# Attention scores taken in pairs of an even and an odd head, with two PSUM banks for each step

## The chip, the cores and the metric

One core of a Trainium2 chip runs the whole program. The metric is the device time of one execution in microseconds (us). Engines are named as the profile names them: PE is the matrix engine (TensorE), DVE the vector engine, ACT the scalar engine, POOL GpSimd, SP the queue that issues the weight loads.

## The reference, cut to what matters

Two layers, 256 tokens, model width 1024, all in float32. In each layer the stretch that concerns us stands between two SwiGLU blocks:

```
h = rms_norm(x);  qa,ka,va, qb,kb,vb, xc,gc = split(h @ w_in)
A: 4 query heads on 2 key/value heads, rotary, window 128, a sink per head
B: 6 heads, rotary, three dilated windows combined by their softmax denominators
C: causal conv(4) -> gated linear recurrence (scan), times gelu(gc)
x = x + concat(A, B, C) @ w_out
```

Heads have 64 channels. Scores are `q . k * 64**-0.5`, masked, and go through a softmax; the mixture of the three windows of B is done with an added mask, so that each head of A and of B needs one score matrix of 256 queries by the keys up to them.

## The kernel before, in words

Weights come from memory as float32 and are split in two parts (`piece`, L128 to L132): ACT writes a rounded part `hi`, DVE the rest `lo`. Each weight product is then three matmuls (hi·hi, hi·lo, lo·hi). There are 7 pairs of such buffers, so a split waits until PE has used an older pair.

The mixing stretch of a layer (`mixer`) is written as a list of steps, `PLAN`, which is walked once per layer. A step `xc`, `qb`, `kb`, `vb`, `pa`, `gc` is a projection by a slice of w_in (`pa` gives q, k and v of A); `cg`, `cs`, `co` are the gates, the scan and the end of C. `B1s0` is the 0th score step of B for the second half of the queries (half 1, which sees 256 keys; half 0 sees 128); `B1p0` multiplies a piece of its softmax by the values; `B1f` divides by the sum and transposes. `woB` and `woCA` are the output projection of the finished parts. A scheduler reorders the instructions of each engine when the program is built, but buffers of one pool are handed out in the order of the list. Once built, the order on each engine is fixed, and each engine takes its instructions in that order.

Scores (`Attend.scores`, L826 to L840): a head's q and k lie transposed, with its 64 channels on one half of the 128 rows, an even head of B on the lower half and an odd one on the upper (for A the two key/value heads). A score step takes up to 512 columns of PSUM, one bank: 2 heads of half 1, or 4 (for B 3) of half 0, all from the same half of the rows. PE writes the scores to the bank; DVE reads it once per head, adds the mask and finds the maximum (L830), which empties the bank; DVE makes the negative maximum (L834 or L836), and ACT the exponential and its sum (L839). `pv` (L850 to L856) transposes the softmax on PE, ACT copies it to SBUF, and PE multiplies by the values into the tile `o`.

PSUM banks: 4 with the tag `mm` (projections, `wout`), 2 with the tag `at` (scores, `o`, one of the three tiles of `xc` and of `gc`, the gates), 2 with the tag `tp` (transposes).

Of the kernel before, what the change touches and what calls it, by code (L numbers as in the profile page):

```python
# [11 lines left out]
F32 = mybir.dt.float32  # L12
F32R = mybir.dt.float32r
I32 = mybir.dt.int32
AF = mybir.ActivationFunctionType
ALU = mybir.AluOpType

P = 128

PLAN = ("xc qb kb cg B1s0 vb B0s0 B0s1 B0p0 B0p1 pa B1s2 B1s1 cs A0s0 B1s3 B1p0 B0f A0s1 B1p2 B1p1 A1s0 B1p3 "  # L20
        "A1s1 A0p1 A0p0 gc A1p0 B1f woB A1p1 A0f A1f co woCA").split()

TAG_GATE, TAG_SCORES, TAG_O, TAG_WO = 'at', 'at', 'at', 'mm'
TAG_XC, TAG_GC = ('mm', 'at', 'mm'), ('at', 'mm', 'mm')

BUFS = 5, 14, 4, 2, 2, 8, 4
# [8 lines left out]
NEG = -3.0e38  # L35
# [3 lines left out]
def hybrid_trunk(ctx: ExitStack, tc: tile.TileContext, a: dict, out: bass.AP):  # L39
    nc = tc.nc  # L40
    x = a["x"]
    S, D = x.shape[1], x.shape[2]
    L = a["w_in"].shape[0]
    DFF = a["ffn1_gate"].shape[2]
    HD = 64
    HF = HD // 2
    AQ, AKV, BH = 4, 2, 6
# [5 lines left out]
    SC = HD ** -0.5  # L53
# [6 lines left out]
    act = ctx.enter_context(tc.tile_pool(name="act", bufs=1))  # L60
# [18 lines left out]
    KC = KD // HC  # L79
# [67 lines left out]
    K = {}  # L147
# [489 lines left out]
    def mixer(l, norm, nxt):  # L637
        V, G, A = nc.vector, nc.gpsimd, nc.scalar
# [5 lines left out]
        NP = BH // 2  # L644
# [70 lines left out]
        n = CT * (S + NTAP)  # L715
# [92 lines left out]
        class Attend:  # L808


            def __init__(self, h, heads, vs, mask, sinks):
                self.h, self.heads, self.vs, self.mask, self.sinks = h, heads, vs, mask, sinks
                self.nk = (h + 1) * P
                self.nh = sum(len(b) for b in heads)
                st = act.tile([P, 4, 8], F32, tag="st", bufs=4, name="st")
                self.mx, self.nm, self.ls, self.ri = (st[:, i] for i in range(4))
                self.slot = [sum(len(b) for b in heads[:i]) for i in range(len(heads))]
                self.sm = [None] * len(heads)
                self.ob = None

            def scores(self, gi):
                group, j, nk, mx, nm = self.heads[gi], self.slot[gi], self.nk, self.mx, self.nm
                h, n = self.h, len(group)
                sb = bank(TAG_SCORES, "scores")
                for s, (i, g, q, k) in enumerate(group):
                    nc.tensor.matmul(sb[:, s * nk:(s + 1) * nk], q[g * HD:(g + 1) * HD, h * P:(h + 1) * P],  # L826
                                     k[g * HD:(g + 1) * HD, :nk], start=True, stop=True)
                sm = act.tile([P, 512], F32, tag="sm", bufs=NSM, name="sm")
                for s in range(n):
                    V.tensor_tensor_reduce(out=sm[:, s * nk:(s + 1) * nk], in0=sb[:, s * nk:(s + 1) * nk],  # L830
                                           in1=self.mask, scale=1.0, scalar=NEG, op0=ALU.add, op1=ALU.max,
                                           accum_out=mx[:, j + s:j + s + 1])
                if self.sinks is None:
                    V.tensor_scalar(nm[:, j:j + n], mx[:, j:j + n], -SC, None, op0=ALU.mult)  # L834
                else:
                    V.scalar_tensor_tensor(nm[:, j:j + n], mx[:, j:j + n], -SC, self.sinks[1][:, j:j + n],  # L836
                                           op0=ALU.mult, op1=ALU.min)
                for s in range(n):
                    A.activation(sm[:, s * nk:(s + 1) * nk], sm[:, s * nk:(s + 1) * nk], AF.Exp, scale=SC,  # L839
                                 bias=nm[:, j + s:j + s + 1], accum_out=self.ls[:, j + s:j + s + 1])  # L840
                self.sm[gi] = sm

            def pv(self, gi):
                h, sm = self.h, self.sm[gi]
                if self.ob is None:
                    self.ob = bank(TAG_O, "o")
                tp = bank("tp", "pT")
                n = len(self.heads[gi]) * self.nk
                for b in range(n // P):
                    nc.tensor.transpose(tp[:, b * P:(b + 1) * P], sm[:, b * P:(b + 1) * P], ident)  # L850
                pT = act.tile([P, 512], F32, tag="pT", bufs=2, name="pT")
                copy("pT", pT[:, :n], tp[:, :n])
                for s, (i, g, q, k) in enumerate(self.heads[gi]):
                    for kb in range(h + 1):
                        b = s * (h + 1) + kb
                        nc.tensor.matmul(self.ob[:, i * HD:(i + 1) * HD], pT[:, b * P:(b + 1) * P], self.vs[kb][i],  # L856
                                         start=(kb == 0), stop=(kb == h))

            def finish(self):
                nh, ls, ri, ob, mx = self.nh, self.ls, self.ri, self.ob, self.mx  # L860
                if self.sinks is not None:
                    V.tensor_tensor(mx[:, :nh], self.sinks[0], self.nm[:, :nh], op=ALU.add)
                    A.activation(mx[:, :nh], mx[:, :nh], AF.Exp)
                    V.tensor_tensor(ls[:, :nh], ls[:, :nh], mx[:, :nh], op=ALU.add)
                V.reciprocal(ri[:, :nh], ls[:, :nh])
                o = scratch(nh * HD, "o")
                order = [i for group in self.heads for i, *_ in group]
                if order == list(range(nh)):
                    V.tensor_tensor(o.rearrange("p (n d) -> p n d", d=HD),
                                    ob[:, :nh * HD].rearrange("p (n d) -> p n d", d=HD),  # L870
                                    ri[:, :nh, None].to_broadcast([P, nh, HD]), op=ALU.mult)
                else:

                    v = lambda z: z[:, :nh * HD].rearrange("p (n g d) -> p g n d", g=2, d=HD)
                    V.tensor_tensor(v(o), v(ob), ri[:, :nh].rearrange("p (g n) -> p g n", g=2)[:, :, :, None]
                                    .to_broadcast([P, 2, nh // 2, HD]), op=ALU.mult)
                return o


# [3 lines left out]
        va, vb = [], []  # L883
# [11 lines left out]
        def a_attend(h):  # L895
            t = C["qkA"]
            heads = [[(g * AG + r_, g, t[:, r_], t[:, AG]) for r_ in range(AG)] for g in range(AKV)]
            sl = slice(l * AQ, (l + 1) * AQ)
            return Attend(h, heads, va, K["mA"][h], (K["sink"][:, sl], K["nsink"][:, sl]))

        def b_in(j):
            dst = QB[j][:, :NP * S].rearrange("p (c t) -> p c t", c=NP)
# [12 lines left out]
        def b_attend(h, q, k):  # L915
            hd = lambda i: (i, i % 2, q[:, i // 2], k[:, i // 2])
            per = 512 // ((h + 1) * P)
            heads = []
            for g in range(2):
                for i0 in range(0, NP, per):  # L920
                    heads.append([hd(2 * i + g) for i in range(i0, min(i0 + per, NP))])
            return Attend(h, heads, vb, K["mB"][h], None)

        def out_stage(ks, last):

            for c in range(HC):
                w = {}
                for k0, n in ks:
                    w.update(zip(range(k0, k0 + n), by_columns(w_out, k0, n, c)))
                n = len(w)  # L930
                w = list(w.items())
                bs = [bank(TAG_WO, "wout")[:, :S] for _ in range(KC)]
                order = [(i, j) for i in range(n - LO) for j in range(KC)]
                order += [(i, j) for j in range(KC) for i in range(n - LO, n)]
# [17 lines left out]

        for step in PLAN:
            nm, arg = step[:2], step[2:]
# [22 lines left out]
            else:  # L977
                g, h = nm[0], int(nm[1])
                t = C[g][h]
# [4 lines left out]
                else:  # L984
                    k, n = R[g]
# [37 lines left out]
```

## Time and profile before

| | |
|---|---|
| three runs | 945.01, 946.7, 946.91 us; median 946.7 |
| the profiled execution | 946.71 us, of which the trace spans 944.9 |
| mean granted clock of PE | 0.996 of full speed |
| PE busy | 935.2 us, 99% |
| DVE, ACT, POOL busy | 662.1 us (70%), 502.0 us (53%), 59.8 us (6%) |
| the two mixing stretches, about | 192 to 293 us and 654 to 755 us |

A busy time is what an engine spent between the start and the end of its instructions. PE's instructions are pipelined: a row of 0.39 us may be followed by the next after 0.23 us, so a cost is best read from one start to the next. [...]

### The profile page before, as it was taken

What the parts mean: (1) busy time and instruction counts of PE and PEld (TensorE: products, weight loads), DVE (VectorE), ACT (ScalarE), POOL (GpSimd) and SP (SyncE); (2) the same over time, 40 slices, a digit from 0 to 9 for tenths busy, and PEclk for the clock granted to TensorE, in tenths of its full rate; (3) what the DMA queues carried; (4) which work ended last, traced back from release to release, by engine and by line L of the source; (5) the groups of instructions that cost most, each with busy time, mean ns of one, the idle gap of its engine ahead of it and who ended that gap; (6) DMA issues with size and microseconds to landing.
All of it is one profiled execution on the core that took longest, in us unless ns stands there. A gap on an engine that the chain in (4) does not pass through costs nothing.

```text
span 944.9 us, 18771 instructions
## 1 busy us (share of the span) xinstructions
PE 935.2 (99%) x7572; PEld 910.7 (96%) x7572; DVE 662.1 (70%) x1155; ACT 502.0 (53%) x769; POOL 59.8 (6%) x107
## 2 busy tenths in 40 slices
PE   8999999999999999999999999999999999999997
PEld 8999999999899999999999999999988999999886
DVE  6786675989678867765577766565995975656544
ACT  7554554455667545555355555544475675555530
POOL 4000001011102000001000000011100100000000
PEclk9999999999999999999999999999999999999999
DMA  8876665655246666565746666654741755666631
GB/s 279 238 227 206 191 197 162 195 175 166 79 132 214 178 205 198 180 216 165 223 157 200 194 205 203 202 180 119 224 138 50 229 178 180 196 207 201 201 112 44
DMA packets 134408, 171.13 MB, mean 181 GB/s; under 512 B 5822, under 2 KB 106258, under 8 KB 134322
## 3 DMA queue, kind: packets, MB, share of 16 engines
q1 hardware_dynamic: 133184, 168.32, 58.0%
q0 software_dynamic: 528, 0.57, 0.4%
q8 instruction: 59, 0.97, 0.4%
q10 hardware_dynamic: 608, 1.06, 0.4%
q14 instruction: 29, 0.22, 0.1%
HBM read 168.88 MB, written 1.05 MB: 180 GB/s over the span
## 4 chain that ended last, share of the span: by engine, by line
PE 97%; issue 1%; DMA 1%; SPq 0%; DVE 0%; POOLq 0%; POOL 0%
PE gate L461 9%; PE gate L462 9%; PE gate L463 8%; PE up L462 8%; PE up L463 8%; PE up L461 8%; PE down L461 6%; PE down L463 6%; PE down L462 6%; PE down L609 2%; PE down L608 2%; PE down L607 2%; PE scores L826 2%; PE wout L938 2%; PE wout L939 2%; PE wout L940 2%
## 5 line engine op out<-in xcount | busy, mean ns | idle before, releaser
L132 DVE TENSOR_TENSOR lo<-raw,hi 128x1024 fp32r<-128x1024 f32 (+2 forms) x334 | 388.8, 1173 | 113.7 <-ACT hi L130 113.3
L130 ACT ACTIVATE hi<-raw 128x1024 fp32r<-128x1024 f32 (+2 forms) x334 | 335.5, 1017 | 167.4 <-PE down L462 60.9
L461 PE MATMUL gate<-x,hi 128*128 128x256 f32 x704 | 195.8, 278 | 0.5 <-ACT x L372 0.5
L462 PE MATMUL gate<-x,hi 128*128 128x256 f32 x704 | 195.1, 277 | 0.0
L461 PE MATMUL up<-x,hi 128*128 128x256 f32 x704 | 194.6, 277 | 0.0
L462 PE MATMUL up<-x,hi 128*128 128x256 f32 x704 | 194.5, 277 | 0.0
L463 PE MATMUL gate<-x,lo 128*128 128x256 f32 x704 | 194.5, 277 | 0.0
L463 PE MATMUL up<-x,lo 128*128 128x256 f32 x704 | 194.1, 276 | 0.0
L461 PE MATMUL down<-g,hi 128*128 128x256 f32 x528 | 145.8, 276 | 0.0
L462 PE MATMUL down<-g,hi 128*128 128x256 f32 x528 | 145.7, 276 | 0.0
L463 PE MATMUL down<-g,lo 128*128 128x256 f32 x528 | 145.6, 276 | 0.0
L461 PEld LDWEIGHTS gate<-x,hi 128*128 128x128 f32 x704 | 132.6, 188 | 0.7 <-ACT x L372 0.7
L462 PEld LDWEIGHTS gate<-x,hi 128*128 128x128 f32 x704 | 132.8, 189 | 0.0
L462 PEld LDWEIGHTS up<-x,hi 128*128 128x128 f32 x704 | 132.4, 188 | 0.0
L463 PEld LDWEIGHTS gate<-x,lo 128*128 128x128 f32 x704 | 132.3, 188 | 0.0
L461 PEld LDWEIGHTS up<-x,hi 128*128 128x128 f32 x704 | 132.3, 188 | 0.0
L463 PEld LDWEIGHTS up<-x,lo 128*128 128x128 f32 x704 | 132.0, 188 | 0.0
L136 ACT ACTIVATE g<-gu 128x256 fp32r<-128x256 f32 x88 | 36.6, 417 | 149.3 <-DVE gu L475 125.4
L461 PEld LDWEIGHTS down<-g,hi 128*128 128x128 f32 x528 | 99.1, 188 | 0.1
L462 PEld LDWEIGHTS down<-g,hi 128*128 128x128 f32 x528 | 99.1, 188 | 0.0
L463 PEld LDWEIGHTS down<-g,lo 128*128 128x128 f32 x528 | 99.0, 188 | 0.0
L474 DVE TENSOR_TENSOR gu<-up,half 128x256 f32<-128x256 f32 x66 | 27.7, 421 | 47.1 <-PE up L463 47.1
(228 smaller groups left out, 1325.5 us busy)
## 6 DMA issues: line engine op xcount, KB each, us to landing
raw<-ffn_down SPq DMA_DIRECT2D x88, 512.0 KB, 4.5
raw<-ffn_gate SPq DMA_DIRECT2D x87, 512.0 KB, 4.7
raw<-ffn_up SPq DMA_DIRECT2D x87, 512.0 KB, 5.2
raw<-w_in SPq DMA_DIRECT2D x40, 384.0 KB, 3.7
raw<-w_out SPq DMA_DIRECT2D x12, 512.0 KB, 3.7
raw<-w_in SPq DMA_DIRECT2D x8, 512.0 KB, 4.6
raw<-w_out SPq DMA_DIRECT2D x8, 256.0 KB, 2.8
xr<-x SPq DMA_DIRECT2D x4, 256.0 KB, 4.6
```

What stands on the lines that cost most here:

```text
L130: nc.scalar.activation(hi[:, :m], raw[:, :m], AF.Copy)
L132: nc.vector.tensor_tensor(lo[:, :m], raw[:, :m], hi[:, :m].bitcast(F32), op=ALU.subtract)
L136: nc.scalar.activation(hi, v, AF.Copy)
L461: nc.tensor.matmul(b, wh, both[:, :S], start=first, stop=False)
L462: nc.tensor.matmul(b, wh, both[:, S:], start=False, stop=False)
L463: return nc.tensor.matmul(b, wl, both[:, :S], start=False, stop=last)
L474: V.tensor_tensor(u, bs[1], half, op=ALU.mult)
L607: nc.tensor.matmul(b, gh, wh, start=first, stop=False)
L608: nc.tensor.matmul(b, gh, wl, start=False, stop=False)
L609: return nc.tensor.matmul(b, gl, wh, start=False, stop=last)
L826: nc.tensor.matmul(sb[:, s * nk:(s + 1) * nk], q[g * HD:(g + 1) * HD, h * P:(h + 1) * P], k[g * HD:(g + 1) * HD, :nk], start=True, stop=True)
L938: nc.tensor.matmul(bs[j], wi, PT[:, k, 0], start=(i == 0), stop=False)
```

## The change

The score step now takes pairs: for each pair of an even and an odd head of B (for A, a head from each key/value head) one score matrix goes to a first bank and the other to a second one, and the matmuls are written alternately, one from the lower half of the rows and one from the upper. Half 1 of B has now 2 steps in place of 4, half 0 has 1 in place of 2, and each half of A has 1 in place of 2: 5 steps a layer in place of 10. Each step asks for two `at` banks at once. The softmax tiles hold the heads in their natural order, so `pv` takes B's half 0 in tiles of 4 and 2 heads, and `finish` needs no reordering. The tile `o` comes from the `mm` banks in place of `at`, and `wout` from two `at` and two `mm` banks in place of four `mm`. `PLAN` is rewritten for the new steps.

```
-PLAN = ("xc qb kb cg B1s0 vb B0s0 B0s1 B0p0 B0p1 pa B1s2 B1s1 cs A0s0 B1s3 B1p0 B0f ...
+PLAN = ("xc qb kb cg B1s0 vb B0s0 B0p0 B0p1 pa B1s1 cs A0s0 B1p0 B0f B1p1 A1s0 B1p2 A0p0 gc ...
-TAG_GATE, TAG_SCORES, TAG_O, TAG_WO = 'at', 'at', 'at', 'mm'
+TAG_GATE, TAG_SCORES, TAG_O, TAG_WO = 'at', 'at', 'mm', ('at', 'at', 'mm', 'mm')
...
             def scores(self, gi):
-                sb = bank(TAG_SCORES, "scores")
-                for s, (i, g, q, k) in enumerate(group):
-                    nc.tensor.matmul(sb[:, s * nk:(s + 1) * nk], q[g * HD:(g + 1) * HD, h * P:(h + 1) * P],
-                                     k[g * HD:(g + 1) * HD, :nk], start=True, stop=True)
...
+                sb = [bank(TAG_SCORES, "scores") for _ in banks]
+                at = {}
+                for s in range(max(len(b) for b in banks)):
+                    for t, group in zip(sb, banks):
+                        if s < len(group):
+                            i, g, q, k = group[s]
+                            at[i] = t[:, s * nk:(s + 1) * nk]
+                            nc.tensor.matmul(at[i], q[g * HD:(g + 1) * HD, h * P:(h + 1) * P],
+                                             k[g * HD:(g + 1) * HD, :nk], start=True, stop=True)
...
+                order = [i for t in tiles for i in t]
+                for i in order:
+                    V.tensor_tensor_reduce(out=p[i], in0=at[i], in1=self.mask, scale=1.0, scalar=NEG, op0=ALU.add,
+                                           op1=ALU.max, accum_out=mx[:, i:i + 1])
...
         def b_attend(h, q, k):
...
+            for i0 in range(0, NP, per):
+                pairs = range(i0, min(i0 + per, NP))
+                banks = [[hd(2 * i + g) for i in pairs] for g in range(2)]
+                idx = range(2 * i0, 2 * pairs[-1] + 2)
+                steps.append((banks, [list(idx[i:i + per]) for i in range(0, len(idx), per)]))
...
-                bs = [bank(TAG_WO, "wout")[:, :S] for _ in range(KC)]
+                bs = [bank(TAG_WO[j], "wout")[:, :S] for j in range(KC)]
```

On PE, where the projection `vb` ends and `pa` follows (the same in both layers), the order changes as follows; `x2` and the like count equal instructions in a row:

```order
 L428 MATMUL vb<-lo,x 128x384
 L430 MATMUL vb<-hi,x 128x384
+L830 MATMUL scores<-mixed 128x256 x4
+L830 MATMUL scores<-mixed 128x128 x6
+L830 MATMUL scores<-mixed 128x256 x2
+L856 MATMUL pT<-ident,sm 128x128 x6
+L862 MATMUL o<-vb,pT 128x64 x4
 L427 MATMUL pa<-hi,x 128x512
 L428 MATMUL pa<-lo,x 128x512
```

All scores of B, the transposes of the softmax of half 0 and four of its value products now stand ahead of the first matmul of `pa`. Before, `pa` followed `vb` at once, and these stood among the matmuls of `pa` and `gc`.

The same place in the changed program, one by one, with the buffers' numbers and with the semaphores that an instruction waits for:

```order
L430 MATMUL vb_2974<-hi_3006,x_2522 128x384
L830 MATMUL scores_2944<-mixed_2597 128x256 [waits DVE_49,Activation_49]
L830 MATMUL scores_2945<-mixed_2597 128x256 [waits Activation_49]
L830 MATMUL scores_2944<-mixed_2597 128x256
L830 MATMUL scores_2945<-mixed_2597 128x256
L830 MATMUL scores_3039<-mixed_2597 128x128 [waits DVE_49]
L830 MATMUL scores_3039<-mixed_2597 128x128 x2
L830 MATMUL scores_3040<-mixed_2597 128x128 [waits DVE_49]
L830 MATMUL scores_3040<-mixed_2597 128x128 x2
L830 MATMUL scores_3187<-mixed_2597 128x256 [waits DVE_49]
L830 MATMUL scores_3188<-mixed_2597 128x256 [waits DVE_49]
```

Three steps of two banks each stand in a row, and there are two `at` banks: the second and the third step wait for DVE to have read the step before. The first step alternates between its two banks, the second was left as three and three.

On PE at the end of `pa`, in both layers:

```order
-L427 MATMUL pa<-hi,x 128x512
-L428 MATMUL pa<-lo,x 128x512
-L850 MATMUL pT<-ident,sm 128x128
-L430 MATMUL pa<-hi,x 128x512
-L850 MATMUL pT<-ident,sm 128x128
+L805 MATMUL qkT<-ident,r 128x128 x3
+L830 MATMUL scores<-mixed 128x128 x4
+L805 MATMUL qkT<-ident,r 128x128 x2
+L856 MATMUL pT<-ident,sm 128x128 x4
+L805 MATMUL qkT<-ident,r 128x128
+L437 MATMUL gT<-ident,o 128x128 x3
+L830 MATMUL scores<-mixed 128x256 x4
```

Before, the projection `gc` began right after `pa` and the transposes `qkT` of A's rotated q and k came some 30 matmuls later. Now `qkT` and the scores of A follow `pa` directly, and `gc` comes behind them.

On DVE in the changed program, between the reading of the first score step and that of the second:

```order
L839 ISA sm_2951,st_2916<-scores_2945,mB1_2235 128x256
L839 ISA st_2916 128x1
L757 TENSOR_TENSOR mixed_2597<-mixed_2597 128x768
L843 TENSOR_SCALAR st_2916<-st_2916 128x4
L760 SCALAR_TENSOR_TENSOR mixed_2597<-mixed_2597 128x256
L760 SCALAR_TENSOR_TENSOR mixed_2597<-mixed_2597 128x256
L839 ISA sm_3047,st_2915<-scores_3039,mB0_2208 128x128
```

L757 and L760 belong to the recurrence of C (L760 is its scan); up to the first reading of scores DVE's order is the same in both programs. What moved here is that two splits of weights (`lo`) that stood among these before now come later.

## Rows read from the trace of the kernel before

**Rows 1.** The page: busy time by engine; the chain that ended last, by engine

```profile
PE 935.2 (99%) x7572; PEld 910.7 (96%) x7572; DVE 662.1 (70%) x1155; ACT 502.0 (53%) x769; POOL 59.8 (6%) x107
PE 97%; issue 1%; DMA 1%; SPq 0%; DVE 0%; POOLq 0%; POOL 0%
```

**Rows 2.** Busy time in a stretch: length, each engine, granted clock, DMA share, GB/s

```profile
230.00:246.00 16.00, 16.00 (x83) 13.00 (x82) 14.52 (x40) 11.25 (x25) 0.73 (x2) 1.00 0.39 122
```

**Rows 3.** Timeline of PE: start, length, engine, line, tiles, shape, count (merged)

```profile
230.04 0.39 PE L427 MATMUL pa<-hi,x 128*128 128x512 f32 x1
...
232.19 1.80 PE L826 MATMUL scores<-mixed 64*128 64x256 f32 x10
233.92 0.51 PE L427 MATMUL pa<-hi,x 128*128 128x512 f32 x1
```

**Rows 4.** Timeline of DVE, first layer

```profile
234.43 0.41 DVE L830 CUSTOM_DVE_ANT_0 sm<-scores,mB 128x256 f32<-128x256 f32 x1
...
234.77 0.41 DVE L830 CUSTOM_DVE_ANT_0 sm<-scores,mB 128x256 f32<-128x256 f32 x1
...
237.74 0.96 DVE L757 TENSOR_TENSOR mixed<-mixed 128x768 f32<-128x768 f32 x1 [0.97 <-ACT mixed L756]
238.61 0.16 DVE L834 TENSOR_SCALAR st<-st 128x3 f32<-128x3 f32 x1
...
239.83 1.84 DVE L760 TENSOR_TENSOR_SCAN mixed<-mixed 128x256 f32<-128x256 f32 x3
241.59 0.26 DVE L830 CUSTOM_DVE_ANT_0 sm<-scores,mB 128x128 f32<-128x128 f32 x1
...
241.78 0.28 DVE L830 CUSTOM_DVE_ANT_0 sm<-scores,mB 128x128 f32<-128x128 f32 x1
```

**Rows 5.** Timeline of ACT, first layer

```profile
243.58 0.40 ACT L839 ACTIVATE sm<-sm,st 128x128 f32<-128x128 f32 x1 [0.84 <-DVE st L834]
...
243.98 0.39 ACT L839 ACTIVATE sm<-sm,st 128x128 f32<-128x128 f32 x1
...
253.09 0.60 ACT L657 ACTIVATE pT<-pT 128x512 f32<-128x512 f32 x1
```

**Rows 6.** Timeline of PE, later in the first layer

```profile
259.19 0.71 PE L826 MATMUL scores<-mixed 64*128 64x128 f32 x4
259.83 0.44 PE L850 MATMUL pT<-ident,sm 128*128 128x128 f32 x2
...
262.14 0.61 PE L850 MATMUL pT<-ident,sm 128*128 128x128 f32 x4
262.68 1.13 PE L826 MATMUL scores<-mixed 64*128 64x256 f32 x4
263.74 1.10 PE L856 MATMUL o<-va,pT 128*128 128x64 f32 x8
```

**Rows 7.** Timelines of PE and DVE, second layer

```profile
692.06 0.39 PE L427 MATMUL pa<-hi,x 128*128 128x512 f32 x1
...
697.85 0.42 DVE L830 CUSTOM_DVE_ANT_0 sm<-scores,mB 128x256 f32<-128x256 f32 x1
```

**Rows 8.** Timeline of DVE, the end of `pa` in the first layer

```profile
243.57 0.35 DVE L661 TENSOR_SCALAR va<-pa,rstd 128x128 f32<-128x128 f32 x1
...
245.01 0.34 DVE L661 TENSOR_SCALAR va<-pa,rstd 128x128 f32<-128x128 f32 x1
...
246.51 1.21 DVE L132 TENSOR_TENSOR lo<-raw,hi 128x1024 fp32r<-128x1024 f32 x1
249.35 0.56 DVE L659 COPY mixed<-qkT 128x384 f32<-128x384 f32 x1 [1.63 <-PE qkT L805]
```

**Rows 9.** Busy time in stretches at the start of the span

```profile
8.00:10.00 2.00, 0.90 (x7) 0.90 (x7) 1.65 (x4) 1.08 (x3) 0.00 (x0) 0.91 0.93 314
10.00:12.00 2.00, 2.00 (x11) 2.00 (x11) 1.80 (x4) 0.84 (x1) 0.00 (x0) 0.50 0.87 261
12.00:14.00 2.00, 2.00 (x15) 2.00 (x15) 2.00 (x3) 2.00 (x6) 0.00 (x0) 0.73 1.09 368
```

More of the change, by code (lines that the diff above doesn't have):

```diff
@@ L18 @@
 P = 128
-PLAN = ("xc qb kb cg B1s0 vb B0s0 B0s1 B0p0 B0p1 pa B1s2 B1s1 cs A0s0 B1s3 B1p0 B0f A0s1 B1p2 B1p1 A1s0 B1p3 "
-        "A1s1 A0p1 A0p0 gc A1p0 B1f woB A1p1 A0f A1f co woCA").split()
-TAG_GATE, TAG_SCORES, TAG_O, TAG_WO = 'at', 'at', 'at', 'mm'
+PLAN = ("xc qb kb cg B1s0 vb B0s0 B0p0 B0p1 pa B1s1 cs A0s0 B1p0 B0f B1p1 A1s0 B1p2 A0p0 gc B1f A1p0 A0f woB "
+        "A1p1 A1f co woCA").split()
+TAG_GATE, TAG_SCORES, TAG_O, TAG_WO = 'at', 'at', 'mm', ('at', 'at', 'mm', 'mm')
 TAG_XC, TAG_GC = ('mm', 'at', 'mm'), ('at', 'mm', 'mm')
@@ L808, in mixer, with __init__ @@
         class Attend:
-            def __init__(self, h, heads, vs, mask, sinks):
-                self.h, self.heads, self.vs, self.mask, self.sinks = h, heads, vs, mask, sinks
+            def __init__(self, h, steps, vs, mask, sinks):
+                self.h, self.steps, self.vs, self.mask, self.sinks = h, steps, vs, mask, sinks
                 self.nk = (h + 1) * P
-                self.nh = sum(len(b) for b in heads)
+                self.nh = sum(len(b) for banks, _ in steps for b in banks)
@@ L815, in __init__ @@
                 st = act.tile([P, 4, 8], F32, tag="st", bufs=4, name="st")
                 self.mx, self.nm, self.ls, self.ri = (st[:, i] for i in range(4))
-                self.slot = [sum(len(b) for b in heads[:i]) for i in range(len(heads))]
-                self.sm = [None] * len(heads)
+                self.sm = []
                 self.ob = None
             def scores(self, gi):
-                group, j, nk, mx, nm = self.heads[gi], self.slot[gi], self.nk, self.mx, self.nm
-                h, n = self.h, len(group)
@@ L824, in scores @@
-                sb = bank(TAG_SCORES, "scores")
-                for s, (i, g, q, k) in enumerate(group):
-                    nc.tensor.matmul(sb[:, s * nk:(s + 1) * nk], q[g * HD:(g + 1) * HD, h * P:(h + 1) * P],
-                                     k[g * HD:(g + 1) * HD, :nk], start=True, stop=True)
[L828 to L832, printed above, removed]
+                (banks, tiles), nk, mx, nm, h = self.steps[gi], self.nk, self.mx, self.nm, self.h
@@ new lines, in scores @@
+                p = {}
+                for tile_heads in tiles:
+                    sm = act.tile([P, 512], F32, tag="sm", bufs=NSM, name="sm")
+                    p.update((i, sm[:, s * nk:(s + 1) * nk]) for s, i in enumerate(tile_heads))
+                    self.sm.append((sm, tile_heads))
+                order = [i for t in tiles for i in t]
+                for i in order:
+                    V.tensor_tensor_reduce(out=p[i], in0=at[i], in1=self.mask, scale=1.0, scalar=NEG, op0=ALU.add,
+                                           op1=ALU.max, accum_out=mx[:, i:i + 1])
@@ L833, in scores @@
+                sl = slice(min(order), max(order) + 1)
                 if self.sinks is None:
-                    V.tensor_scalar(nm[:, j:j + n], mx[:, j:j + n], -SC, None, op0=ALU.mult)
+                    V.tensor_scalar(nm[:, sl], mx[:, sl], -SC, None, op0=ALU.mult)
                 else:
[L836 to L840, printed above, removed]
@@ L841, in scores @@
-                self.sm[gi] = sm
+                    V.scalar_tensor_tensor(nm[:, sl], mx[:, sl], -SC, self.sinks[1][:, sl], op0=ALU.mult, op1=ALU.min)
+                for i in order:
+                    A.activation(p[i], p[i], AF.Exp, scale=SC, bias=nm[:, i:i + 1], accum_out=self.ls[:, i:i + 1])
             def pv(self, gi):
-                h, sm = self.h, self.sm[gi]
+                h, (sm, heads) = self.h, self.sm[gi]
                 if self.ob is None:
@@ L847, in pv @@
                 tp = bank("tp", "pT")
-                n = len(self.heads[gi]) * self.nk
+                n = len(heads) * self.nk
                 for b in range(n // P):
@@ L852, in pv @@
                 copy("pT", pT[:, :n], tp[:, :n])
-                for s, (i, g, q, k) in enumerate(self.heads[gi]):
+                for s, i in enumerate(heads):
                     for kb in range(h + 1):
@@ L866, in finish @@
                 o = scratch(nh * HD, "o")
[L867 to L876, printed above, removed]
+                V.tensor_tensor(o.rearrange("p (n d) -> p n d", d=HD),
+                                ob[:, :nh * HD].rearrange("p (n d) -> p n d", d=HD),
+                                ri[:, :nh, None].to_broadcast([P, nh, HD]), op=ALU.mult)
                 return o
@@ L898, in a_attend @@
             sl = slice(l * AQ, (l + 1) * AQ)
-            return Attend(h, heads, va, K["mA"][h], (K["sink"][:, sl], K["nsink"][:, sl]))
+            per = 512 // ((h + 1) * P)
+            return Attend(h, [(heads, [list(range(i, i + per)) for i in range(0, AQ, per)])], va, K["mA"][h], (K["sink"][:, sl], K["nsink"][:, sl]))
         def b_in(j):
@@ L917, in b_attend @@
             per = 512 // ((h + 1) * P)
[L918 to L922, printed above, removed]
+            steps = []
+            for i0 in range(0, NP, per):
[3 more added lines that the diff above has]
+                steps.append((banks, [list(idx[i:i + per]) for i in range(0, len(idx), per)]))
+            return Attend(h, steps, vb, K["mB"][h], None)
         def out_stage(ks, last):
```

## The prediction

> **What bounds the kernel now.** I read the page first. PE is busy 99% of the span, and the chain that ended last runs on PE for 97% of it [rows 1]. The busy time by stretch says the same of the place of the change: from 230 to 246 us PE is busy 16.00 of 16.00 us at a granted clock of 1.00, while DVE is busy 14.52 [rows 2]. So whatever shortens PE's own work is gained in full, whatever makes PE wait is lost in full, and DVE is nearly full just where the scores begin. The timelines of PE and DVE show how these two stand to each other. PE ends `vb` and starts `pa` at 230.04 us, and makes the first scores of B at 232.19 [rows 3]; DVE reads the first of these only at 234.43 [rows 4], because it is behind. In the second layer `pa` starts at 692.06 and DVE reads the first scores at 697.85 [rows 7]. Before, PE had the matmuls of `pa` and `gc` to go on with, so that this lag cost nothing. DVE's order up to that first reading is the same in the changed program, and what it works on there comes from before the end of `vb`; so I keep 234.43 and 697.85 as the times at which it can start to empty the first score banks, however early PE fills them.
>
> **What PE's own work loses.** A score run of four records takes 0.64 us with 128 columns and 1.06 us with 256 [rows 6], and the run of 4 wide and 6 narrow records 1.73 us, from 232.19 to 233.92 [rows 3]. The three together give 0.112 us a narrow record, 0.217 a wide one and 0.19 fixed for a run. Ahead of the run at 262.68, four transposes of 0.11 us from 262.14 would have been over at 262.58, so another 0.1 is lost on entering. About 0.3 us for a run, then. Before there are 9 runs a layer (the first holds two steps); the order now shows 3. Six fewer, in two layers: 12 x 0.3 = 3.6 us saved. The number of scores, transposes and value products is unchanged, and I cost the moves of `o` and `wout` between banks at nothing: in the output projection no wait of PE is seen before, and the chain from the last `gc` to the split of C has all of `woB` to hide behind. If that cover failed it would cost under 1 us a layer.
>
> **The first wait it adds.** Between `vb` and `pa`, PE now has three score steps, six transposes and four value products in a row, and only two `at` banks. Counted from T, the first reading by DVE, the chain to the first matmul of `pa` is: four readings of wide scores at 0.34 us, 1.37 from start to start [rows 4]; L757, 0.87, and a small operation, 0.1; two scans at 1.76 / 3 = 0.59, 1.17; three readings of narrow scores at about 0.2, 0.6 (the first bank of the second step is free); the third scan, 0.59; three more readings, 0.6; the negative maximum, 0.2. DVE is done with the second step at T + 5.5. ACT then makes six exponentials at 0.40, 2.4, and copies the first four transposed tiles, 0.60 [rows 5]; PE makes four value products in eight records of 0.11, 0.9 (eight in 1.10 with the tail [rows 6]). Sum 9.4, with the hand-overs 9.5. `pa` starts at 234.43 + 9.5 = 243.9, in place of 230.04: 13.9 us later. In these PE does 2.0 us (first step), 1.6 (second), 1.15 (third), 0.66 (transposes) and 0.9 (values) = 6.3. It idles 7.6 us. In the second layer T is 5.79 us behind the end of `vb`, in place of 4.39, and the idle time is 9.0. Behind the waiting scores stand all of `pa` and `gc`, whose weights are there: nothing of this can be taken ahead, since PE takes its list in order.
>
> **The second wait.** Behind `pa` there is no more `gc` to go on with. The transposes of A's q and k need the rotation, and A's scores need DVE's copy of them. DVE begins as the first half of `pa` is done, about 0.5 us before the end of all (the last record of that half stands four places from the end at 0.23, and lasts 0.39). Then it has scaling and rotation of the first half, 1.44 us (243.57 to 245.01), of the second, 1.4, a split, 1.2, which stands between them, and the copy, 0.56 [rows 8]: 4.6. A's first scores come 4.1 us after the end of `pa`, and PE has 0.33 us of transposes in that time: 3.8 idle. Then PE waits again, for the bank of the transposes, behind four readings, two small operations and a copy on DVE, 1.9 us, with 0.8 of its own work: 1.1 idle. Together 4.9 a layer. After that A's wide scores, `gc` and the values are ready when PE comes to them.
>
> **Sum at full clock.** (7.6 + 4.9) + (9.0 + 4.9) - 3.6 = +22.8 us.
>
> **The clock.** PE has hardly waited in this kernel, and there is one place that shows what a wait does: at the start of the span. In 8 to 10 us PE is busy 0.90 of 2 us, the granted clock falls to 0.50 (1.2 in place of 2.4 GHz), and stays there through 12 us and part of 12 to 14 although PE is busy throughout [rows 9]: (0.09 x 2 + 0.50 x 2 + 0.27 x 2) / 0.5 = 3.4 us at half clock, 1.7 us of work lost. The four new gaps are emptier than that stretch (PE works 6.3 of 13.9 us in the first). I take one such fall for each: 4 x 1.7 = +6.8. From below it is 0, if the work scattered in the gaps holds the clock. From above the clock is low through most of each gap, and then the value products, A's scores and the transposes that stand on the chain take double, some 1.6 us more a gap: +13.
>
> **The two halves of the rows.** No row of before shows a matmul on one half directly behind one on the other. The nearest rows are records of one half that follow each other at 0.112 and 0.217, and I take these: nothing gained. If a change of half costs as much as entering a run, 0.3, it is three changes in each of A's two steps, +1.8 a layer, +3.6. If two halves run at the same time, eight records take the time of five: A's steps lose 0.34 and 0.65 us, -2.0 in both layers. For B's steps either is nothing, since PE then waits for DVE at a time that DVE's list sets. The Trainium skill has a rule on this ("TensorEngine Tiling (Array Packing)", Key Properties): different tiles of the array load weights and multiply in parallel. By that rule the pairs overlap, which is the third rival below; no run here shows it yet.
>
> **Forecast.** 22.8 + 6.8 = +29.6 us on the profiled execution's 946.71 us, which is the median of the runs shown (946.7): 976.
>
> **Rivals.**
> - The clock holds. For it: PE is not wholly idle in the gaps. Against it: rows 9. 946.7 + 22.8 = 969.5, or 967.5 with overlapping halves.
> - The clock is low through the gaps: 946.7 + 22.8 + 13 = 982.5; with costly changes of half 986.
> - The clock falls as forecast and the halves overlap: 974.
> - Not slower: PE's saving outweighs the waits. Its place is the start of `pa`: for that DVE would have to reach the first scores as PE ends them and hand both banks back within what is saved, 3.6 us plus 6.5 if all 40 scores overlapped (half of 13.1 us: 40 wide and 40 narrow records at 0.217 and 0.112). It decides if all waits of the two layers together stay under 10 us, where I count 26.4; the time would then be 937 to 947. Against it, even from T = 231.9, when the first step ends, the chain of 9.5 us stands, and it has the rows of before in every term.
> - The change doesn't wholly do what it says: the second step of B stands as three and three in the order, not alternating. That costs nothing here, for the reason above.
>
> **How the numbers follow.** Forecast 0.48; clock holds 0.17; clock low throughout 0.15; overlap with falling clock 0.14; not slower 0.06, of which 0.04 below 944.8, 0.01 within 0.2% of 946.7 (the least that a measurement of this kernel can tell from no change) and 0.01 just above. So faster 0.04, same 0.01, slower 0.95. The range goes from 964 (clock holds, halves overlap, and the chain 10% shorter than I add it up) to 986.
>
> **What would show it.** Right: PE's busy share falls to about 96%; its waits name DVE readings of scores at score lines and ACT exponentials at the transposes; in the first layer `pa` starts near 244 us and in the second about 15 us behind the end of `vb`; DVE reads the first score at 234.4; A's scores start some 4 us behind `pa`; the granted clock is 0.50 for a few us in four places. Wrong: `pa` starts within 4 us of the end of `vb`; DVE reads the first scores much before 234; the mixing stretches are not longer by about 12 us each and the difference sits elsewhere. Alternating records of A that start less than 0.11 (narrow) or 0.21 us (wide) apart on average would show the halves overlapping.

## The result, and the profile after

The changed kernel takes 980.2 us (median of 4 runs, 979.56 to 981.2) where the kernel before, beside it, takes 946.8 (945.01 to 947.58): a ratio of 1.0359, 95% interval [1.0333, 1.0385]. It is slower by 33.4 us. The forecast was 976, the 946.71 us of the profiled execution and 29.6 more. Of the executions below, one is set aside: the profiled one of kernel 12 took 959.88 us, where its others took 942.4 to 948.7; its median below counts it, its ratio does not.

I read the page first: the busy times and the chain by engine, which answer to [rows 1].

```profile
PE 949.3 (97%) x7572; PEld 920.3 (94%) x7572; DVE 663.3 (68%) x1145; ACT 501.6 (51%) x765; POOL 60.6 (6%) x107
PE 94%; DVE 3%; issue 1%; DMA 1%; ACT 0%; POOL 0%; SPq 0%; POOLq 0%; DVEq 0%; ACTq 0%
```

PE has the same 7572 instructions, is busy 14 us longer and still has a smaller share of the span. So there are two losses: it waits, and its work takes longer. DVE, which had 0% of the chain, has 3% of it. The waits of PE (line, who releases it: us in all, times, longest) say where:

```profile
PE scores L830 <- DVE st L839: 11.6, 4, 5.4
PE qkT L805 <- POOL r L795: 5.8, 2, 2.9
```

The timeline of PE in the first layer, which answers to [rows 3, 6]:

```profile
230.41 1.14 PE L830 MATMUL scores<-mixed 64*128 64x256 f32 x8
235.51 2.34 PE L830 MATMUL scores<-mixed 64*128 64x128 f32 x12 [3.97 <-DVE st L839]
238.99 2.43 PE L830 MATMUL scores<-mixed 64*128 64x256 f32 x4 [1.14 <-DVE st L839]
241.35 1.98 PE L856 MATMUL pT<-ident,sm 128*128 128x128 f32 x6
243.34 1.97 PE L862 MATMUL o<-vb,pT 128*128 128x64 f32 x8
245.06 0.77 PE L427 MATMUL pa<-hi,x 128*128 128x512 f32 x1
...
261.13 0.74 PE L805 MATMUL qkT<-ident,r 128*128 128x128 f32 x3 [2.91 <-POOL r L795]
262.52 1.23 PE L830 MATMUL scores<-mixed 64*128 64x128 f32 x8 [0.65 <-DVE mixed L659]
```

`vb` ends at 230.3, and `pa`, which followed at once, starts at 245.06. A score or value product of the order lists stands in the trace as two records, so the first step's four are eight. Three things are to be seen. Eight wide records take 1.14 us, where four took 1.13 [rows 6]: the two halves of the rows run at the same time. The next step waits 3.97 us for DVE. And from then on everything is slow: six transposes take 1.98 us, where the kernel at full clock makes four in 0.61 [rows 6]. DVE's own rows, to be held against [rows 4]:

```profile
234.69 0.41 DVE L839 CUSTOM_DVE_ANT_0 sm<-scores,mB 128x256 f32<-128x256 f32 x1
...
240.18 0.17 DVE L843 TENSOR_SCALAR st<-st 128x6 f32<-128x6 f32 x1
```

DVE reads the first score at 234.69, though PE had it ready some 4 us earlier; it was 234.43 before. How long the clock is down is seen in the four stretches around the gaps (columns as in [rows 2]):

```profile
234.57:248.23 13.66, 11.57 (x38) 8.28 (x39) 6.92 (x34) 8.50 (x28) 0.00 (x0) 0.50 0.06 19
261.88:275.53 13.65, 12.35 (x57) 10.58 (x58) 5.77 (x27) 5.84 (x22) 1.06 (x2) 0.50 0.11 38
712.44:729.50 17.06, 12.54 (x40) 9.04 (x41) 9.36 (x37) 8.50 (x28) 0.00 (x0) 0.50 0.11 38
743.16:753.40 10.24, 9.46 (x44) 7.68 (x45) 4.85 (x25) 3.19 (x12) 0.56 (x2) 0.50 0.09 34
```

That is 54.6 us at 0.50 (1.2 in place of 2.4 GHz), and each stretch reaches well past its gap: the first lasts 3.2 us into `pa`, whose records start 0.43 us apart there in place of 0.23.

The whole loss lies between the end of `vb` and the last `wout` of each layer. Here are these two stretches and their sum, of the kernel before and then of the changed one:

```profile
230.04:293.42 63.38, 63.38 (x460) 57.30 (x460) 49.60 (x127) 40.08 (x90) 7.34 (x9) 1.00 0.42 130
sum 126.76, PE 126.76 PEld 114.61 DVE 100.12 ACT 80.39 POOL 14.69; mean PE 63.38 PEld 57.30 DVE 50.06 ACT 40.20 POOL 7.34
```

```profile
230.31:310.63 80.32, 70.99 (x460) 62.93 (x460) 48.65 (x118) 39.03 (x85) 6.27 (x7) 0.83 0.32 96
709.21:790.05 80.84, 70.11 (x460) 61.92 (x460) 49.66 (x119) 39.27 (x86) 6.26 (x7) 0.83 0.34 102
sum 161.16, PE 141.10 PEld 124.85 DVE 98.30 ACT 78.31 POOL 12.52; mean PE 70.55 PEld 62.43 DVE 49.15 ACT 39.15 POOL 6.26
```

The two stretches grow by 34.40 us (the span by 34.5, 944.9 to 979.4). Of these PE idles 161.16 - 141.10 = 20.06, and its 460 instructions a layer take 14.34 longer, in both layers together. The same sum is made for every kernel below.

### The profile page after: what moved, and what is told of

It reads as the page before. It is cut to its first block, busy times and chain, and to the rows that moved or that the text cites. A ratio compares the mean times of both kernels' runs of the same rounds, so it can differ in the third digit from the quotient of the medians.

```text
span 979.4 us, 18748 instructions
## 1 busy us (share of the span) xinstructions
PE 949.3 (97%) x7572; PEld 920.3 (94%) x7572; DVE 663.3 (68%) x1145; ACT 501.6 (51%) x765; POOL 60.6 (6%) x107
## 4 chain that ended last, share of the span: by engine, by line
PE 94%; DVE 3%; issue 1%; DMA 1%; ACT 0%; POOL 0%; SPq 0%; POOLq 0%; DVEq 0%; ACTq 0%
PE gate L461 8%; PE up L461 8%; PE gate L462 8%; PE gate L463 8%; PE up L462 8%; PE up L463 8%; PE down L461 6%; PE down L463 6%; PE down L462 6%; PE down L609 2%; PE down L608 2%; PE down L607 2%; PE o L862 2%; PE wout L940 2%; PE wout L942 1%; PE wout L941 1%
```

## The experiments

In the table, the stretches are the two from the end of `vb` to the last `wout`, of the profiled execution; idle is their sum less PE's busy time. In kernels 5 and 9 PE's busy time holds the fillers, 16.15 and 17.57 us.

| kernel | median, us | ratio to before, 95% | stretches | PE busy | idle |
|---|---|---|---|---|---|
| before | 946.8 | | 126.76 | 126.76 | 0 |
| changed | 980.2 | 1.0333 to 1.0385 | 161.16 | 141.10 | 20.06 |
| 1 `o` in mm, no pairs | 992.4 | 1.0437 to 1.0561 | 173.55 | 154.30 | 19.25 |
| 2 `pa` first | 969.6 | 1.0207 to 1.0279 | 151.26 | 142.84 | 8.42 |
| 3 `gc` first | 975.6 | 1.0264 to 1.0338 | 156.11 | 140.44 | 15.67 |
| 4 both first | 946.0 | 0.9963 to 1.0009 | 125.29 | 119.75 | 5.54 |
| 5 gaps filled | 972.3 | 1.0272 to 1.0298 | 153.79 | 145.82 | 7.97 |
| 6 early `gc` | 954.5 | 1.0074 to 1.0101 | 136.18 | 129.97 | 6.21 |
| 7 the same, not alternating | 958.4 | 1.0123 to 1.0149 | 138.43 | 132.23 | 6.20 |
| 8 changed, not alternating | 980.8 | 1.0360 to 1.0387 | 162.65 | 143.34 | 19.31 |
| 9 gaps filled more | 972.3 | 1.0273 to 1.0322 | 152.48 | 145.07 | 7.41 |
| 10 both first, late gelu | 956.4 | 1.0101 to 1.0128 | 138.44 | 126.31 | 12.13 |
| 11 the same, no pairs | 961.7 | 1.0158 to 1.0191 | 142.37 | 132.06 | 10.31 |
| 12 both first, copies on DVE | 945.2 | 0.9977 to 1.0007 | - | - | - |

Beside the kernels 1 to 12 the kernel before took 945.2 to 945.9 us.

The theory: the pairs as such save PE time, and the loss comes from what they force. They need both `at` banks, so `o` moves to `mm`; the `mm` banks are handed out in the order of the list, so `pa` and then `gc` get theirs only behind value products that wait for DVE and ACT. The rival: the pairs are the cost.

**1. The bank alone.** The kernel before, with one word changed.

```
-TAG_GATE, TAG_SCORES, TAG_O, TAG_WO = 'at', 'at', 'at', 'mm'
+TAG_GATE, TAG_SCORES, TAG_O, TAG_WO = 'at', 'at', 'mm', 'mm'
```

> The kernel before with one edit: the value products `o` take an mm bank in place of an at bank. No pairs, all nine score runs as before. Theory (the loss comes from the order that the banks force: `pa` and `gc` get their mm banks only after B's and A's value products have theirs): `pa` starts some 10 to 16 us behind the end of `vb` in both layers, and the time is 965 to 990 us. Rival (the loss comes from making the scores in pairs, from the two-bank steps or the alternation): within 0.5% of the kernel before, 942 to 951.

Measured 992.4. Its PE timeline has the same hole in front of `pa`, made of single-bank steps:

```profile
228.69 1.80 PE L826 MATMUL scores<-mixed 64*128 64x256 f32 x10
232.93 0.93 PE L826 MATMUL scores<-mixed 64*128 64x128 f32 x6 [2.44 <-DVE st L830]
234.43 2.07 PE L826 MATMUL scores<-mixed 64*128 64x256 f32 x6 [0.57 <-DVE st L830]
237.47 2.40 PE L850 MATMUL pT<-ident,sm 128*128 128x128 f32 x6 [0.96 <-ACT sm L839]
239.77 1.54 PE L856 MATMUL o<-vb,pT 128*128 128x64 f32 x6
241.07 0.77 PE L427 MATMUL pa<-hi,x 128*128 128x512 f32 x1
```

`pa` starts 12.5 us behind the end of `vb` in place of at once. The time is 2.4 us above the range of the theory, the start of `pa` within it. The rival is out: the bank of `o` costs 46.9 us by itself, more than the whole change. What the pairs, the new list and the banks of `wout` together take back of it, some 12 us, was not separated.

**2 to 4. Cover for the waits.** In the changed kernel's list `pa` is moved to stand behind B's first score step `B1s0` and ahead of its second (2), `gc` ahead of A's steps (3), or `pa` as in 2 and `gc`, with the scan `cs`, ahead of B's value products (4).

```
2: ... B1s0 vb pa B0s0 B0p0 B0p1 B1s1 cs A0s0 B1p0 B0f B1p1 A1s0 B1p2 A0p0 gc B1f ...
3: ... B1s0 vb B0s0 B0p0 B0p1 pa B1s1 gc cs A0s0 B1p0 B0f B1p1 A1s0 B1p2 A0p0 B1f ...
4: ... B1s0 vb pa B0s0 cs gc B0p0 B0p1 B1s1 A0s0 B1p0 B0f B1p1 A1s0 B1p2 A0p0 B1f ...
```

> The changed kernel with `pa` moved ahead of B's first score step in the list; everything else of the change stays. Theory (the first wait is a hole that `pa` would have covered): `pa` starts as `vb` ends, the first wait with its half clock goes in both layers, and 16 to 22 us of the 33.4 come back: 958 to 965. The second wait stays. Rival (PE would wait for DVE at this point whatever stands there, so the hole only moves behind `pa` and adds to the second wait): 975 to 981.

> The changed kernel with `gc` moved ahead of A's steps in the list; `pa` still stands behind B's value products. Theory (the second wait, 4.9 us of idle time a layer by the prediction and its half clock, is covered by `gc`): 10 to 15 us come back, 965 to 971; the first wait stays as it was. Rival (the second wait only moves behind `gc`, to A's last steps, which then have nothing to hide behind): 977 to 983.

> The changed kernel with `pa` ahead of B's first score step and `gc` ahead of B's value products, so that both waits are covered by the two projections; pairs, alternation and banks as changed. Theory (two waits and their half clock are the whole loss): between 944 and 952, with some us lost in the tail of A, which has no `gc` to cover it any more. If the two covers simply add: 980.2 less 16 to 22 less 10 to 15, so 943 to 954. Rival (the hole is DVE's backlog and only moves): above 965.

Measured 969.6, 975.6 and 946.0: 10.6, 4.6 and 34.2 us back. Only 4 lies in the range of its theory; 2 and 3 lie between theory and rival. In kernel 2 the first wait is gone and does not move, as the theory says: the idle time falls from 20.06 to 8.42 us. But the second wait is still there behind `pa`, it brings the clock down, and B's later scores, transposes and values, which `pa` now precedes, are made at half clock behind it. PE's busy time rises from 141.10 to 142.84:

```profile
244.56 0.74 PE L804 MATMUL qkT<-ident,r 128*128 128x128 f32 x3 [2.75 <-POOL r L794]
246.02 0.66 PE L804 MATMUL qkT<-ident,r 128*128 128x128 f32 x2 [0.71 <-POOL r L794]
```

```profile
246.00:262.00 16.00, 15.88 (x52) 11.60 (x53) 5.58 (x31) 6.72 (x28) 0.38 (x1) 0.50 0.06 22
```

Two waits, of 2.75 and 0.71 us, and all of the next 16 us run at 0.50. In kernel 3 the second wait is covered, but in the first layer PE then waits 0.94 us for DVE and 0.63 for ACT among A's steps, and the clock is at 0.50 for 20 us behind that: that layer's stretch is 80.23 us, where it was 80.32, and all that comes back lies in the second layer, 75.88 in place of 80.84. Only with both waits covered does the clock hold; 10.6 and 4.6 add to 15, both together give 34. In kernel 4:

```profile
228.20:290.84 62.64, 59.90 (x460) 54.53 (x460) 48.04 (x118) 39.49 (x86) 6.31 (x7) 1.00 0.41 124
sum 125.29, PE 119.75 PEld 109.00 DVE 96.93 ACT 79.25 POOL 12.60; mean PE 59.88 PEld 54.50 DVE 48.46 ACT 39.62 POOL 6.30
```

This also gives what the pairs are worth: at full clock PE's work is 59.88 us a layer in place of 63.38, 7.0 less in both. The scores alone (busy time of that tile in the two stretches) make 6.7 of it; the sums before and here:

```profile
sum 126.76, PE 17.84 PEld 11.71 DVE 12.48; mean PE 8.92 PEld 5.86 DVE 6.24
```

```profile
sum 125.29, PE 11.14 PEld 7.01 DVE 12.09; mean PE 5.57 PEld 3.50 DVE 6.04
```

But 5.54 us of idle time stand against it, and the median is not told apart from the kernel before. The largest part is B's value products, which wait for a copy on ACT behind `gc`'s gelu and its table load:

```profile
260.08 1.10 PE L861 MATMUL o<-vb,pT 128*128 128x64 f32 x8 [1.57 <-ACT pT L656]
```

**5 and 9. The clock by itself.** The changed kernel with transposes that nobody reads in the gaps, so that PE is busy while the real work waits as before.

```
+        def fill(n):
+            ps = bank("tp", "dm")
+            with behind(C["lm"]):
+                for i in range(n):
+                    nc.tensor.transpose(ps[:, i % 4 * P:(i % 4 + 1) * P], ident, ident)
```

> The changed kernel with transposes of the identity matrix, which nobody reads, put into the gaps so that PE is not idle there: 30 behind B's first score step, 9 behind its second, 25 behind `pa`. The order of the real work, the waits for DVE and POOL and the banks stay, so the waits themselves are no shorter. Theory (the forecast's 6.8 us for the clock was too little: the clock at 0.50 for 54.6 us costs 10 to 14 us on the path, the waits at full clock some 20): the granted clock is 1.00 through the gaps, and the time is 966 to 971. Rival (the clock is low where PE only waits anyway and costs next to nothing; the loss is all in the waits): 978 to 983.

> The kernel with transposes in the gaps, with more of them: 33 (in the second layer 47) behind B's first score step, 10 behind its second, 25 behind `pa`. In the kernel with 30, 9 and 25 the clock was still at 0.50 for 20.5 us in place of 54.6, and the time 7.8 us lower than the changed kernel's; at that rate, 0.23 us of time for one us at half clock, the rest is worth 4.7 us. Theory (the waits alone cost what the forecast's sum at full clock says, with the halves overlapping: 946.7 + 22.8 - 2.0 = 967.5, and the clock the rest): clock 1.00 in all four gaps and 966 to 970. Rival (the rest of the half clock lies where PE waits anyway): 971 to 974.

Measured 972.3 both times. The first fill was expected at 966 to 971 and ends between theory and rival; the second lies in the range of its rival, and 5 us expected back from it did not come. Here is each layer of kernel 9 up to the end of `pa` and from there on, then the busy time of the fillers alone:

```profile
228.71:256.45 27.74, 26.33 (x135) 20.81 (x135) 14.42 (x44) 13.20 (x34) 0.00 (x0) 0.88 0.20 59
256.45:304.46 48.01, 45.90 (x395) 43.92 (x394) 33.81 (x75) 25.75 (x52) 6.27 (x7) 1.00 0.40 127
703.04:731.55 28.51, 26.74 (x148) 21.48 (x148) 15.57 (x45) 13.38 (x35) 0.00 (x0) 0.94 0.19 57
731.55:779.77 48.22, 46.11 (x395) 44.13 (x394) 33.82 (x75) 25.75 (x52) 6.27 (x7) 1.00 0.43 138
sum 152.48, PE 145.07 PEld 130.33 DVE 97.62 ACT 78.09 POOL 12.54; mean PE 36.27 PEld 32.58 DVE 24.40 ACT 19.52 POOL 3.13
```

```profile
sum 152.48, PE 17.57 PEld 16.42; mean PE 8.79 PEld 8.21
```

The changed kernel up to the end of `pa`:

```profile
230.31:258.06 27.75, 22.63 (x91) 16.91 (x90) 14.55 (x44) 13.20 (x34) 0.00 (x0) 0.75 0.20 58
709.21:738.84 29.63, 23.11 (x91) 17.25 (x90) 15.58 (x45) 13.44 (x35) 0.00 (x0) 0.71 0.19 56
```

So 10 us are left at half clock, of 54.6 (twice 27.74 x 0.12 and 28.51 x 0.06), and the stretches are 8.7 us shorter (161.16 to 152.48; the medians differ by 7.9). Of the 8.7, 7.6 lie behind `pa`, where the clock is now at 1.00 throughout; up to the end of `pa` the first layer gains nothing. What is left at half clock lies there, at the last transposes, B's value products and the start of `pa`:

```profile
239.17 2.40 PE L855 MATMUL pT<-ident,sm 128*128 128x128 f32 x6 [1.08 <-ACT sm L846]
241.57 1.97 PE L861 MATMUL o<-vb,pT 128*128 128x64 f32 x8
...
715.09 2.25 PE L855 MATMUL pT<-ident,sm 128*128 128x128 f32 x6
```

The waits, idle plus fillers, are 7.41 + 17.57 = 25.0 us in kernel 9. The real work is 145.07 - 17.57 = 127.5, 7.8 above kernel 4's. The half clock explains at most 5 of it. Some 3 are a wait that counts as busy: the six transposes take 2.40 and 2.25 us in place of 0.82 in kernel 4, because they come one by one behind exponentials that start 0.39 us apart on ACT. Whether the fillers themselves delay the rest was not separated.

**6 to 8. What alternating is worth.** Kernel 6 has `pa` where kernel 2 has it, makes the first block of two of `gc`'s tiles early, so that `gc` has its banks, and keeps the rest as cover; 7 and 8 are kernel 6 and the changed kernel without the alternation.

```
6:    ... B1s0 vb pa ga B0s0 B0p0 B0p1 B1s1 cs A0s0 ...
    +            elif nm == "ga":
    +                c_gate(True)
...
7, 8:
    -                for s in range(max(len(b) for b in banks)):
    -                    for t, group in zip(sb, banks):
    +                for t, group in zip(sb, banks):
    +                    for s in range(len(group)):
                             if s < len(group):
```

> The changed kernel with `pa` ahead of B's first score step, and the first block of two of `gc`'s three tiles made there too, so that `gc` has its two mm banks before the value products ask for theirs; the rest of `gc` keeps its late place in the list and is taken wherever PE would wait. Theory (the loss is in the order alone, and pairs save PE time once both waits are covered): 3.6 us for twelve score runs less and 2 to 6 us for the halves that run at the same time, so 937 to 943, faster than both kernels. Rival (what the pairs save is lost again in waits for the exponentials at the value products, as in the kernel with both projections ahead): 944 to 949.

> The kernel with the early block of `gc`, with each step's scores made first all of one half of the rows, then all of the other, in place of alternating; pairs, steps and banks the same. Theory (alternating halves run at the same time; 40 wide and 40 narrow records in the two layers' A steps and B steps take half as long): 3 to 6 us slower than with alternation. Rival (what is saved is the fixed cost of a score run alone, and the halves do not matter): within 1 us of the kernel with alternation.

> The changed kernel without the alternation: each step's scores first all of one half of the rows, then all of the other. Theory (in B's steps the end is set by DVE, so only A's steps lose, and those are made at half clock): 1 to 4 us slower than the changed kernel, 981 to 984. Rival (alternation is worth as much here as where PE does not wait): 3 to 7 us slower, 983 to 987.

Measured 954.5, 958.4 and 980.8. Kernel 6 fails both of its ranges: its `gc` is used up by 261 us, and B's last and A's first value products then wait with nothing left to go on with, until the clock falls again, to 0.50 for 10 us:

```profile
264.06 1.10 PE L879 MATMUL o<-vb,pT 128*128 128x64 f32 x8 [0.96 <-ACT pT L656]
266.70 1.97 PE L879 MATMUL o<-va,pT 128*128 128x64 f32 x8 [1.53 <-ACT pT L656]
```

Kernel 7 is 3.8 us slower than 6, in the range of its theory, but not by its mechanism: the scores take 14.28 us in kernel 6 and 14.94 in kernel 7. Of the 2.25 us by which the two profiled executions differ in the stretches, 1.8 lie in the second layer, where the clock is at 0.50 for 6.7 us in kernel 7 and 3.3 in kernel 6. Without alternation the first step still takes 1.14 us; of the steps whose two halves follow each other directly only the narrow one grows, from 0.94 to 1.26. B's third step and A's come apart in both kernels, with other work between their parts, and show nothing here. The rows in kernel 7:

```profile
232.19 1.14 PE L847 MATMUL scores<-mixed 64*128 64x256 f32 x8
243.11 1.26 PE L847 MATMUL scores<-mixed 64*128 64x128 f32 x12
```

So the halves run at the same time where one follows the other directly: in blocks of two wide scores as well as in turn, in blocks of three narrow ones in part (one behind the other, 12 x 0.112 + 0.19 = 1.53 by the prediction's fit). In the changed kernel alternating changes nothing that can be measured: 980.8 against 980.2, ratios of 1.0374 and 1.0359; both ranges expected for kernel 8 began higher.

**10 to 12. A version that beats both?** Kernel 10 is kernel 4 with the gelu held behind the last exponential, 11 the same without pairs, 12 is kernel 4 with three copies of transposed tiles a layer on DVE.

```
10: +            with behind(C["lx"]):
    +                A.activation(C["ge"], C["ge"], AF.Gelu_apprx_tanh)
12: -                copy("pT", pT[:, :n], tp[:, :n])
    +                copy("pV" if (len(self.vs[0]), h, gi) in ((6, 1, 1), (6, 1, 2), (4, 0, 0)) else "pT", ...)
```

> The kernel with `pa` ahead of B's first score step and `gc` ahead of B's value products, with one more edit: the gelu of `gc` is held behind the last exponential, so that ACT's two table loads (1.28 us each) and the gelu (0.84) no longer stand ahead of the exponentials that PE's value products wait for. Theory (in that kernel the gain of the pairs, 3.6 us for the runs and some 4 for the halves, is eaten by waits of 2.5 us a layer behind that ACT work): the waits shrink to under 1 us a layer and the time is 938 to 943, faster than the kernel before. Rival (ACT's exponentials and copies alone are as long as the wait, whatever the gelu does): 943 to 947.

> The kernel before, without pairs, in the list order of the late-gelu kernel: `o` in an mm bank, `pa` ahead of B's second score step, `gc` ahead of B's value products, gelu behind the last exponential; nine score runs of one bank a layer as before. Theory (pairs save PE 7 to 8 us in two layers when nothing waits): 6 to 12 us slower than the late-gelu kernel. Rival (in a kernel whose waits are covered the pairs change nothing): within 3 us of it.

> The kernel with `pa` ahead of B's first score step and `gc` ahead of B's value products, with three of the copies of transposed tiles a layer (B's last two of the second half and A's first) made by DVE in place of ACT, which there stands behind table loads and exponentials while DVE is idle. In that kernel PE's value products wait 3.8 us for these copies, 1.57 and 0.31 a layer, and PE's work is 3.5 us a layer less than before. Theory (those copies are what is left of the waits): 1 to 4 us less, 941 to 945, faster than the kernel before by 0.1 to 0.5%. Rival (the wait only moves to the exponentials, one engine earlier): 945 to 948, not told apart from the kernel before.

Measured 956.4, 961.7 and 945.2. Kernel 10 misses both of its ranges and is worse than 4: the gelu did not leave the chain but moved to where A's last copy stands behind it, with a table load on both sides (timeline of ACT, then the wait on PE):

```profile
263.35 1.28 ACT L771 ACT_TABLE_LOAD   x1
264.65 0.84 ACT L771 ACTIVATE ge<-ge 128x768 f32<-128x768 f32 x1
265.51 1.28 ACT L871 ACT_TABLE_LOAD   x1
266.80 0.20 ACT L871 ACTIVATE st<-st 128x4 f32<-128x4 f32 x1
266.91 0.58 ACT L656 ACTIVATE pT<-pT 128x512 f32<-128x512 f32 x1
```

```profile
267.54 1.97 PE L864 MATMUL o<-va,pT 128*128 128x64 f32 x8 [3.03 <-ACT pT L656]
```

Beside it the pairs are worth 5.3 us (961.7 less 956.4), just below the 6 to 12 expected; the scores differ by 5.6 us. Kernel 12 is in the range of its rival, not told apart from the kernel before. Of its executions, those with a mean clock of 0.998 or 0.999 take 942.4 to 943.3 us and those with 0.991 to 0.995 take 945.2 to 948.7; kernel 4 spreads from 943.0 to 947.6 in much the same way, with one exception (946.2 at 0.999). The kernel before took 944.6 to 945.7 beside kernel 12 where its mean clock was 0.998 or 0.999, so at that clock kernel 12 is some 2 us faster; since these executions are picked by their clock, this is a hint and not a result. Whether what is left of the waits brings the clock down in some executions was not tested. No version beats the kernel before by more than can be measured.

## Why the prediction was right, and which terms were not

The forecast was a sum of three terms on the profiled execution. Each can now be held against a run.

- **The first wait, its place and start: right.** DVE reads the first score at 234.69 (forecast 234.43), in the second layer 5.79 us behind the end of `vb` (forecast 5.79). `pa` starts at 245.06, where 244 was forecast, and in the second layer 16.2 us behind `vb` in place of about 15; the 1 us more fits the value products at half clock. Kernel 1 shows the cause to be the order of the banks, and kernel 4 that the wait goes when the list gives `pa` and `gc` their banks earlier.
- **The second wait: right in place, a little large.** A's first scores start 4.3 us behind the end of `pa` (4.1 forecast), held by DVE's copy and by a sum on POOL, which the forecast did not name. The wait for the bank of the transposes is 0.65 and not 1.1.
- **Both waits together: about right.** 26.4 us were forecast. Kernel 9, where the clock nearly holds, has 25.0, or 28 with the transposes that come one by one behind the exponentials; 1.2 of these are waits of `wout`, which the forecast put at nothing with under 1 us a layer as its bound. In the changed kernel only 20.06 are seen as idle, because slow work fills part of the same gaps.
- **PE's own work: mis-sized.** The forecast took -3.6 us from the score runs and nothing from the halves. Kernel 4 has -7.0. The rival of overlapping halves was true: [rows 3, 6] give eight wide records 1.93 us one behind the other (8 x 0.217 + 0.19), and they take 1.14. The Trainium skill ("TensorEngine Tiling (Array Packing)", Key Properties) has different tiles load weights and multiply in parallel; the trace agrees (eight records in 1.14 us), and kernel 7 shows that wide scores need no strict turn.
- **The clock: mis-sized, and the larger miss.** "I take one such fall for each: 4 x 1.7 = +6.8" is the step that failed. It took the fall at the start of the span [rows 9], 3.4 us long, for the typical one; here the stretches at 0.50 last 10.2 to 17.1 us. Its reading that the gaps are emptier than that stretch does not hold for the first: 6.3 of 13.9 us are 45%, as are 0.90 of 2. With PE's work at -7.0 and the waits at 28, the clock has 34.4 + 7.0 - 28 = 13.4 us left to explain. Filling the gaps gave back 8.7 of these. The 10 us still at half clock cost some 4 more by the rows: the values take 1.97 and 1.72 us in place of 1.10, and `pa` runs at half clock for 3.4 and 2.1 us. This is an estimate, since no run has the clock at 1.00 in all four gaps; it comes near the +13 that the prediction gave as its bound from above.

- **The marks named ahead.** PE's share is 97%, 96 were named; the waits name DVE's readings at the scores, but ACT's exponentials at no transpose, since PE at half clock comes to these late (in kernel 9 one waits 1.08 us); the stretches grow by 17 us each and not by 12. The forecast's own sum would have been 14.8 each: the 12 leaves its term for the clock out.

By terms: -3.4 (work), +1.6 (waits), +6.6 (clock, the remainder) make +4.8, the difference of 34.4 from the forecast's 29.6. The path was right; that the time came out so near is in part luck, since the two misses partly cancel. The combination that held is "the clock is low through the gaps" with overlapping halves: 982.5 less 2.0 is 980.5, measured 980.2. The rival on the other side fell at its own condition: all waits under 10 us were asked, 20 to 25 are there.

## What to carry to other kernels

Before a tile moves to another pool of banks, list who is handed banks of that pool behind it: here one word moved two projections behind chains on DVE and ACT and cost 46.9 us. On an engine that is busy throughout, price a new wait twice, as idle time and as the slow work that follows it, and expect a cover to pay in full only when the other waits of the stretch are covered too, as here. A saving on the bound engine, real as it is (7 us here), is gained only if the other engines' results still come in time.

## What the runs showed of the hardware

- Scores on different halves of PE's rows overlap within one run of instructions: eight wide records in 1.14 us, as long as four of one half (1.13), alternating or in blocks of two scores; twelve narrow ones in 0.94 us alternating and 1.26 in blocks of three.
- Waits of 2.75 and 0.71 us in a stretch that is otherwise busy were followed by 16 us at half clock (kernel 2), although PE was busy for 15.88 of them.
- Waits of 1.57, 0.31 and 0.65 us within 5 us (kernel 4) left the clock at 1.00 in the profiled execution; in kernel 6, 0.96 and 1.53 within 4 us did not.
